# A two-layer mLSTM/attention backbone on one core: TensorE's order written by the program's own plan instead of by the scheduler

## The chip, the core and the metric

The kernel runs on one core of one Trainium2 chip. TensorE (PE) multiplies matrices, VectorE (DVE), ScalarE (ACT) and GpSimd (POOL) work on rows, SyncE (SP) issues the DMAs; each engine has its own list of instructions, and semaphores tie the lists together. Matrix products are accumulated in PSUM, of which the kernel's pools take eight banks; the other tiles lie in SBUF. The metric is the device time of one execution in microseconds, the median of several runs. One further execution was recorded by the profiler; its rows are quoted below.

## The reference

One step through two layers (`DEPTH = 2`), for 128 context tokens and 512 latent tokens with the same weights. D is 1024. Per layer:

```python
sh_a, sc_a, g_a, sh_m, sc_m, g_m = split(silu(cond) @ w_ada + b_ada, 6)
h = x * (1 + sc_a) + sh_a
mq, mk, mv, mo, mg, sq, sk, sv, nq, nk, nv = split(h @ w_in + b_in)
y_ml  = mlstm(mq, mk, mv, mg) normalised, * norm_g * sigmoid(mo)   # 4 heads, two directions
y_swa = softmax with a sink logit over a window and 256 cached keys @ v  # 6 heads, rotary q and k
y_nat = softmax(q k * scale + bias) over an 8x32 patch and 256 cached keys @ v  # 6 heads
x = layer_norm(ALPHA * x + g_a * (concat(y_ml, y_swa, y_nat) @ w_out)) * ln1_g + ln1_b
h = x * (1 + sc_m) + sh_m
x = layer_norm(ALPHA * x + g_m * (square(relu(h @ w_mlp1)) @ w_mlp2)) * ln2_g + ln2_b
```

Context tokens attend to context tokens only. Besides x, the new keys, values and mLSTM states of the context are outputs.

## The kernel before

**Tiling.** The 640 tokens are five tiles of 128 (`NT = 5`; tile 0 is the context). Each large product is made of three matmuls: an operand is split into a rounded part and the remainder (`piece`, L249 to L256: an ACT cast at L254 and a DVE subtraction at L255), and hi·hi, lo·hi and hi·lo are added in PSUM. There are two forms. `gemm_tok` (L258) keeps a tile of the activations stationary, 24 matmuls per token tile into a bank `gtok` (L270). `gemm_feat` (L283) keeps the weights stationary and sends 320 tokens through, twice 24 matmuls into `gfeat` (L301).

**Small matmuls that use part of the array.** These matter for the change. `score` (L751, matmul L758, `s`) works on the two row halves of the array (64x128), one head each. `pv` (L777) turns the softmaxed block `P` with PE transposes (L790, `ptp`), copies the result out of PSUM to `PT`, the first and third group of four on DVE (L799), the second on ACT (L801), and then multiplies it with the values in the two column halves (128x64, L805, `o`), one head each. `ada` (L163, matmul L137, `adaps`) makes the adaLN rows in four column quarters (128x32), four matmuls at a time. In the mLSTM `mls` and `upd` use halves too. The program writes the matmuls of the two heads, and of the four quarters, in turn, so that neighbours work on different parts of the array. An `o` matmul in fp32 is two records of the trace, so a group of 8 shows as 16.

**The plan.** Attention blocks, the mLSTM's blocks and state chain, the transposes of the next stage's input (`to_feat`, L337, transposes L347, `pth`), the outputs of the keys, and `ada` are generators in a queue (`add`, `pump`, `q`, L60 to L95). After every six matmuls of a large product `q` moves a clock of the program forward and takes steps from the queue whose delay has passed. At most two attention blocks are open (`WINDOW`). `drain` empties the queue before the next stage. The order that comes out is only the order in which the code is written: a scheduler then reorders every engine, PE too, by its own priorities.

**Stages of a layer** (`layer`, L1050): the mLSTM's projections (`proj_ml`), three token projections (`proj_tok_a`, `_b`, `_c`), the gates and the mLSTM, then for u = 0, 1, 2 the key and query projections of two heads of neighbourhood attention (`nat`) and of windowed attention (`swa`), each followed by adding five blocks to the queue: 30 softmax blocks a layer. Their projections (`gfeat`) are the filler between the blocks. `tail1` (L937) is the output projection, in `gemm_tok`, with residual and LayerNorm (`ln_add` L920 and L924, `ln_stats` L926 to L934); `to_feat` of each tile follows after a delay of 9.85 in the plan. LayerNorm's gain and bias on the residual (`ln_out`, L968 and L969, whole 1024-wide rows on DVE) come with `ln_late` while the next stage begins. `mlp` (L978) is four chunks of eight `gemm_feat` and two `gemm_tok`. The end of `mlp` of layer 0 crosses to layer 1 in the same way as `tail1` crosses to `mlp`.

**PSUM.** Pool `gp` has four banks for the large products, `sp` one buffer of two banks for scores, `tp` one bank for transposes, `op` one for `o` and the mLSTM.

## Time and profile before

| | us |
|---|---|
| median of 3 runs | 1769.1 (1766.75 to 1769.91) |
| the profiled execution's own time | 1767.37 |
| its span, first instruction to last | 1765.6 |
| PE busy | 1709.0 (97%) |
| DVE busy | 987.7 (56%) |
| ACT busy | 637.6 (36%) |
| TensorE's granted clock, mean | 0.991 |

The stages are found in the trace by the lines of PE's instructions, and the stretches used below follow them: start and first projections of layer 0 up to 200 us, most of its attention 200 to 390, the output projection from 390, its crossing to the MLP 417 to 451, the MLP 451 to 891, the crossing to layer 1 905 to 942, layer 1's attention 1075 to 1265, its crossing 1280 to 1305 and its MLP to 1748. PE counts as busy also while a matmul takes longer than its neighbours of the same shape, so a busy PE is not an engine at its peak: the time between the starts of successive rows tells more than the busy share.

### The profile page before, as it was taken

The numbers are of one execution on the slowest core, as the hardware profiler recorded it, in microseconds if no ns is written. First come the engines' busy times: TensorE is split into PE (matmuls) and PEld (weight loads), VectorE is DVE, ScalarE is ACT, GpSimd is POOL, SyncE is SP. The second block draws the span as 40 slices with busy tenths as digits, with TensorE's granted clock in tenths as the row PEclk, the third lists the DMA queues.
The fourth block names the chain that finished last, engine by engine and source line by source line (L and its number), as shares of the span: only waits on it lengthen the run. The fifth ranks groups of instructions, "written<-read, shape, count | busy, mean of one in ns | idle before, by whom it ended". The sixth has DMA issues, their size and how long they took to land.

```text
span 1765.6 us, 27638 instructions
## 1 busy us (share of the span) xinstructions
PE 1709.0 (97%) x10708; PEld 1441.4 (82%) x10708; DVE 987.7 (56%) x2147; ACT 637.6 (36%) x1410; POOL 182.5 (10%) x152
## 2 busy tenths in 40 slices
PE   6999999999999999999999999999999999999996
PEld 3778777777978978879879798777789898898985
DVE  2368667768533243234384698777784333423438
ACT  2333445534522313213244335565263142231420
POOL 0142000000200201101100411000002011020110
PEclk9999999999999999999999899999999999999998
DMA  8646433233334444434223252211422131221312
GB/s 276 203 129 199 160 98 114 78 119 116 110 106 148 143 137 155 132 109 158 72 89 115 61 170 72 61 59 61 132 92 89 48 108 57 93 78 48 102 43 83
DMA packets 106000, 195.24 MB, mean 111 GB/s; under 512 B 16490, under 2 KB 43114, under 8 KB 100748
## 3 DMA queue, kind: packets, MB, share of 16 engines
q1 hardware_dynamic: 105868, 193.47, 34.1%
q8 instruction: 84, 1.38, 0.3%
q14 instruction: 48, 0.39, 0.1%
HBM read 185.16 MB, written 8.26 MB: 110 GB/s over the span
## 4 chain that ended last, share of the span: by engine, by line
PE 86%; DVE 9%; DMA 2%; issue 1%; ACT 1%; SPq 1%; POOL 0%; DVEq 0%; POOLq 0%
PE gfeat L301 37%; PE gtok L270 32%; PE o L805 4%; PE s L758 4%; PE ptp L790 3%; PE adaps L137 3%; PE mli L609 1%; DVE wst L255 1%; DMA adab<-in_b_ada 1%; DVE res L968 1%; DVE Xt L352 0%; PE pth L347 0%; DMA Dt<-md 0%; DVE res L969 0%; DMA md<-mscr 0%
## 5 line engine op out<-in xcount | busy, mean ns | idle before, releaser
L301 PE MATMUL gfeat<-Xt,wst 128*128 128x320 f32 x4416 | 704.1, 315 | 8.6 <-ACT Xt L211 3.8
L301 PEld LDWEIGHTS gfeat<-Xt,wst 128*128 128x128 f32 x4416 | 655.9, 190 | 47.7 <-issue 25.3
L270 PE MATMUL gtok<-wst,f1T 128*128 128x512 f32 x1920 | 451.5, 395 | 0.0
L270 PEld LDWEIGHTS gtok<-wst,f1T 128*128 128x128 f32 x1920 | 358.7, 188 | 92.8 <-issue 9.2
L255 DVE TENSOR_TENSOR wst<-wrawt,wst 128x512 fp32r<-128x512 f32 (+2 forms) x392 | 271.6, 700 | 270.1 <-ACT wst L254 269.3
L254 ACT CAST wst<-wrawt 128x512 fp32r<-128x512 f32 (+2 forms) x392 | 233.8, 603 | 516.9 <-PE gtok L270 217.0
L920 DVE TENSOR_TENSOR gtok<-gtok,row 128x512 f32<-128x512 f32 x100 | 69.5, 697 | 229.4 <-PE gtok L270 227.6
L997 POOL TENSOR_TENSOR f1T<-f,f1T 128x640 fp32r<-128x640 f32 x64 | 100.8, 1575 | 900.9 <-ACT f1T L996 900.9
L270 PE MATMUL gtok<-wst,Xt 128*128 128x384 f32 (+1 forms) x720 | 129.5, 331 | 1.3 <-DVE wst L255 1.3
L270 PE MATMUL gtok<-wst,yT 128*128 128x512 f32 x480 | 125.1, 405 | 0.0
L270 PEld LDWEIGHTS gtok<-wst,Xt 128*128 128x128 f32 x720 | 114.4, 191 | 9.6 <-issue 3.6
L992 ACT COPY f<-gfeat 128x320 f32<-128x320 f32 x128 | 54.3, 427 | 168.4 <-PE gfeat L301 164.5
L270 PEld LDWEIGHTS gtok<-wst,yT 128*128 128x128 f32 x480 | 86.7, 188 | 22.4 <-issue 4.1
L769 ACT ACTIVATE P<-P,nm 128x512 f32<-128x512 f32 (+2 forms) x120 | 80.6, 673 | 28.8 <-DVE nm L765 16.1
L993 DVE SCALAR_TENSOR_TENSOR f<-f 128x640 f32<-128x640 f32 x64 | 52.7, 824 | 53.2 <-ACT f L992 53.2
L763 DVE TENSOR_REDUCE nm<-P 128x2 f32<-128x1024 f32 (+2 forms) x60 | 66.0, 1107 | 19.6 <-ACT P L892 8.3
L790 PE MATMUL ptp<-ident,P 128*128 128x128 f32 x432 | 71.2, 281 | 2.9 <-DVE P L774 1.8
L137 PE MATMUL adaps<-adaw,cs 128*32 128x512 f32 (+1 forms) x576 | 67.0, 483 | 6.1 <-DVE grow L502 4.2
L790 PEld LDWEIGHTS ptp<-ident,P 128*128 128x128 f32 x432 | 49.0, 140 | 19.2 <-issue 5.7
L350 ACT ACTIVATE val<-pth,affB,affA 128x128 f32<-128x128 f32 x120 | 45.3, 461 | 52.2 <-PE pth L347 51.0
L996 ACT CAST f1T<-f 128x640 fp32r<-128x640 f32 x64 | 46.6, 728 | 31.6 <-DVE f L993 31.6
L799 DVE COPY PT<-ptp 128x512 f32<-128x512 f32 (+1 forms) x72 | 43.1, 599 | 22.4 <-PE ptp L790 22.3
(207 smaller groups left out, 1349.8 us busy)
## 6 DMA issues: line engine op xcount, KB each, us to landing
wrawt<-in_w SPq DMA_DIRECT2D x256, 256.0 KB
adaw<-in_w_ada SPq DMA_DIRECT2D x40, 1024.0 KB
wrawt<-in_w_f SPq DMA_DIRECT2D x56, 256.0 KB
adaw<-in_w_ada SPq DMA_DIRECT2D x32, 256.0 KB
wrawt<-in_w_o SPq DMA_DIRECT2D x32, 256.0 KB
Dt<-md SPq DMA_DIRECT2D x40, 128.0 KB
nbias<-in_nbias SPq DMA_DIRECT2D x18, 256.0 KB
row<-adar SPq DMA_DIRECT2D x8, 512.0 KB
```

Of the source, the lines that this page charges most:

```text
L137: self.nc.tensor.matmul(ps[32 * j : 32 * j + 32, :], lhsT=self.cs[:, k, :], rhs=w[:, j, :], start=(k == 0), stop=(k == 7))
L254: nc.scalar.copy(ws[:, 0, :], raw)
L255: nc.vector.tensor_tensor(out=ws[:, 1, :], in0=raw, in1=ws[:, 0, :].bitcast(F32), op=ALU.subtract)
L270: nc.tensor.matmul(o, lhsT=A[k][:, hl, t * 128 : (t + 1) * 128], rhs=ws[k][:, wl, :], start=(cnt == 0), stop=(cnt == 23),)
L301: nc.tensor.matmul(g[i, h], lhsT=w[i][k // 4][:, wl, (k % 4) * 128 : (k % 4 + 1) * 128], rhs=self.Xt[:, k, hl, h * 320 : (h + 1) * 320], s ...
L758: nc.tensor.matmul(out[h], lhsT=qt[r, a, q0 : q0 + 128], rhs=kf(r, b), start=(i == 0), stop=(i == 2))
L763: nc.vector.tensor_reduce(out=nm[:, 0:2], in_=P[:, :, 0:nk], axis=AX.X, op=ALU.max, negate=True)
L769: nc.scalar.activation(P[:, h, 0:nk], P[:, h, 0:nk], AF.Exp, bias=nm[:, h : h + 1], accum_out=nm[:, 2 + h : 3 + h])
L790: nc.tensor.transpose(pt[:, j, :], P[:, h, i * 128 : (i + 1) * 128], self.ident)
L805: nc.tensor.matmul(o[64 * h : 64 * h + 64, :], lhsT=vf(h, i), rhs=PT[:, h, i, :], start=(i == 0), stop=(i == n - 1))
L920: nc.vector.tensor_tensor(out=o, in0=o, in1=gr[:, qs], op=ALU.mult)
L997: nc.gpsimd.tensor_tensor(out=y[:, 1], in0=f, in1=y[:, 0].bitcast(F32), op=ALU.subtract)
```

## The change

**Order.** The layers are built under `tc.manual_schedule(engines={PE})`: PE keeps the order in which the program writes its instructions. The other engines are still ordered by the scheduler.

**The plan.** `add` and the generators now work with a time at which a step is ready, and `use(engine, us)` books time on a list for ACT, DVE or POOL and returns when the work ends there. `free` waits in the plan until the booked reader of a PSUM bank is done. A step is only written into PE's order after that time. mLSTM blocks run in the order 0, 2, 3, 1, 4 with their normalisation in a group of its own, `fin`. Attention's projections wait for `live` tiles (`until`).

**PSUM and SBUF.** `gp` 4 to 3 banks, `tp` 1 to 2; `upd` and both scores `s2` use `tp`; the pool `ptp` goes and `pp` has four buffers for P and PT.

**Attention.** Every copy to PT is made by ACT. Keys of windowed attention are projected first, `swa` comes ahead of `nat` in each u, `proj_tok_c` after the first `swa`, from which on three attention blocks may be open.

**Output projection.** Its first half goes block by block over y (`by_block`, in the order `YORDER`), tiles 0 to 2 in `gp` and then 3 and 4 in the banks of the scores; there is no drain ahead of it. LayerNorm's gain and bias are made in halves by `ln_half`, at two points within the next stage, in place of `ln_late`. `ada` is spaced 9.5 instead of 12 or 14; the first adaLN bias is loaded ahead of the first weights, and later ones lie in the buffer of the adaLN weights.

The two orders hold the same 9760 matmuls. Counted over them, PE goes from one array shape to another (whole array, row halves, column halves, quarters) 630 times before and 364 times after; in the first stage, up to the first `gtok`, 51 and 9 times. A pair of matmuls on different halves is torn apart by another kind of instruction at 49 places fewer in `o`, about 55 fewer in scores and mLSTM; 8 groups of four of `adaps` are no longer torn.

First place: PE in layer 0's attention, while the projections of u = 1 run. `s` are scores, `ptp` transposes of P, `o` the products with the values, `gfeat` the projections. Before:

```order
L758 MATMUL s<-qkt 128x256 x6
L758 MATMUL s<-kc,qkt 128x256 x6
L301 MATMUL gfeat<-Xt,wst 128x320 x18
L790 MATMUL ptp<-ident,P 128x128 x4
L137 MATMUL adaps<-adaw,cs 32x512 x4
L758 MATMUL s<-qkt 128x256 x6
L790 MATMUL ptp<-ident,P 128x128 x4
L805 MATMUL o<-PT,vt 64x128
L758 MATMUL s<-kc,qkt 128x256 x5
L805 MATMUL o<-PT,vt 64x128 x2
L790 MATMUL ptp<-ident,P 128x128 x4
L805 MATMUL o<-PT,vt 64x128
```

and the same kinds of blocks after:

```order
L375 MATMUL gfeat<-Xt,wst 128x320 x12
L945 MATMUL o<-PT,sv 64x128 x4
L945 MATMUL o<-PT,vc 64x128 x4
L169 MATMUL adaps<-adaw,cs 32x512 x4
L375 MATMUL gfeat<-Xt,wst 128x320 x12
L886 MATMUL s<-qkt 128x128 x6
L375 MATMUL gfeat<-Xt,wst 128x320 x6
L886 MATMUL s<-qkt 128x256 x6
L886 MATMUL s<-kc,qkt 128x256 x6
L375 MATMUL gfeat<-Xt,wst 128x320 x12
L929 MATMUL ptp<-ident,P 128x128 x2
```

The scores, products and adaLN groups stand whole, and the large product comes in runs of 6, 12 or 18 between them.

Second place: PE where layer 0's attention opens. Before, its first block stands among matmuls of the projections:

```order
L156 MATMUL adapt<-ident,adab 128x128 x4
L137 MATMUL adaps<-adaw,cs 32x512 x3
L301 MATMUL gfeat<-Xt,wst 128x320
L758 MATMUL s<-qkt 128x128 x6
L301 MATMUL gfeat<-Xt,wst 128x320 x23
L790 MATMUL ptp<-ident,P 128x128 x2
L301 MATMUL gfeat<-Xt,wst 128x320 x6
```

After, with `mli` the inner products of the mLSTM, `pty` the transposes of its result and `ptko` that of a key output:

```order
L375 MATMUL gfeat<-Xt,wst 128x320 x24
L756 MATMUL pty<-ident,hs 128x128 x2
L886 MATMUL s<-qkt 128x128 x6
L169 MATMUL adaps<-adaw,cs 32x512 x4
L706 MATMUL mli<-vaug,Dt 128x65 x4
L712 MATMUL mli<-mlst,mq 128x130 x4
L706 MATMUL mli<-vaug,Dt 128x65 x4
L863 MATMUL ptko<-ident,kx 128x128
L929 MATMUL ptp<-ident,P 128x128 x2
L886 MATMUL s<-qkt 128x256 x6
L886 MATMUL s<-kc,qkt 128x256 x6
L945 MATMUL o<-PT,sv 64x128 x2
```

From the run of 24 on no large product stands in PE's order for 35 rows, while four softmax blocks and two mLSTM blocks open and close; layer 1 has a like stretch.

Third place: DVE where `tail1` of layer 0 crosses to the MLP; `res` is the residual, `Xt` the next input. Before:

```order
L920 TENSOR_TENSOR gtok<-gtok,row 128x512
L352 TENSOR_TENSOR Xt<-val,Xt 128x4x128
L924 SCALAR_TENSOR_TENSOR res<-res,gtok 128x512
L968 TENSOR_TENSOR res<-res,row 128x1024
L926 BN_STATS bst<-res 128x6
L352 TENSOR_TENSOR Xt<-val,Xt 128x4x128
L932 BN_AGGR bmv<-bst 128x2
L969 TENSOR_TENSOR res<-res,row 128x1024
```

After:

```order
L1084 TENSOR_TENSOR gtok<-gtok,row 128x512
L1088 SCALAR_TENSOR_TENSOR res<-res,gtok 128x512
L426 TENSOR_TENSOR Xt<-val,Xt 128x4x128
L1090 BN_STATS bst<-res 128x6
L291 TENSOR_TENSOR wst<-wrawt,wst 128x512
L1096 BN_AGGR bmv<-bst 128x2
L291 TENSOR_TENSOR wst<-wrawt,wst 128x512
```

The 1024-wide gain and bias are gone from here; their halves (`lnrow`) follow after the last tile's statistics.

The diff, cut:

```diff
+    def use(self, eng, us, after=None):
+        t = (self.T if after is None else after) + 0.08
+        plan = self.te[eng] = [p for p in self.te[eng] if p[1] > self.T - 10.0]
+        while us > 0.01:
+            d = min(us, 0.7)
+            for i, (a, b) in enumerate(plan):
+                if a - t >= d:
+                    break
+                t = max(t, b)
+            else:
+                i = len(plan)
+            plan.insert(i, (t, t + d))
+            t, us = t + d, us - d
+        return t
...
-                        cost, delay = next(s[0])
+                        cost, ready = next(s[0])
                         self.T += cost
-                        s[2] = self.T + delay
+                        s[2] = max(self.T, ready)
...
+    def free(self, *names):
+        while max(self.busy[n] for n in names) > self.T:
+            yield 0.0, max(self.busy[n] for n in names)
...
-    def softmax(self, P, nk, sink=None):
+    def softmax(self, P, nk, f, sink=None):
...
+        f = self.use("V", 0.1 + 1.1 * w, f)
         nc.vector.tensor_reduce(out=nm[:, 0:2], in_=P[:, :, 0:nk], axis=AX.X, op=ALU.max, negate=True)
...
-        yield 0.0, 3.0
+        yield 0.0, f - 0.4 * w
...
-            if gi % 2 == 0:
-                nc.vector.tensor_copy(dst, src)
-            else:
-                nc.scalar.copy(dst, src)
-            yield 0.11 * len(grp), 0.5
+            nc.scalar.copy(dst, src)
+            f = self.use("A", 0.12 + 0.115 * len(grp), self.T + 0.11 * len(grp) + 0.25)
+            self.busy["t"] = f
+            yield 0.11 * len(grp), (f if gi == len(groups) - 1 else f - 0.6 if gi == 1 else self.T) + 0.1
+        yield from self.free("o")
...
+        def finish(t, hs):
...
+            f = self.use("V", 6.0, f)
...
+        bt = self.ada_bias(0, 0, 0, 512)
         load(0)
         nc.sync.dma_start(self.ident, I["ident"])
         self.layer_consts(0)
-        bt = self.ada_bias(0, 0, 0, 512)
...
+            for k in range(7):
+                blocks(k, range(3))
+            self.until(lambda: self.s_left == 0)
...
+            s = self.sp.tile([128, 2, 512], F32, tag="s", name="gtok")
+            g += [s[:, 0], s[:, 1]]
+            for k in range(7):
+                blocks(k, range(3, NT))
+            blocks(7, range(NT))
...
-                    self.add(self.to_feat(r, t, A, B, lg, lb, None), "feat", 9.85)
+                    self.add(self.to_feat(r, t, A, B), "feat", self.use("V", 2.5, f) + (0.5 if t < 3 else 5.0))
...
-            self.gemm_tok([self.Y[k] for k in YORDER], I["w_o"][l, q], 512, ev(q))
+            self.gemm_tok(self.Y, I["w_o"][l, q], 512, ev(q), by_block=q == 0)
...
-    for l in range(L):
-        net.layer(l)
+    with tc.manual_schedule(engines={mybir.EngineType.PE}):
+        for l in range(L):
+            net.layer(l)
```

## Rows read from the trace of the kernel before

**Rows 1.** The page, parts 1 and 4: busy time and chain of waits.

```profile
PE 1709.0 (97%) x10708; PEld 1441.4 (82%) x10708; DVE 987.7 (56%) x2147; ACT 637.6 (36%) x1410; POOL 182.5 (10%) x152
...
PE 86%; DVE 9%; DMA 2%; issue 1%; ACT 1%; SPq 1%; POOL 0%; DVEq 0%; POOLq 0%
```

**Rows 2.** Stretches: length; busy PE, PEld, DVE, ACT, POOL (instructions); clock; DMA share, GB/s.

```profile
0.00:59.00 59.00, 41.78 (x384) 26.11 (x384) 18.10 (x50) 13.97 (x24) 6.54 (x9) 1.00 0.78 260
...
200.00:390.00 190.00, 188.64 (x1417) 139.97 (x1417) 136.92 (x304) 97.30 (x253) 5.97 (x4) 1.00 0.31 102
...
417.00:451.00 34.00, 30.88 (x170) 26.63 (x169) 29.72 (x67) 23.89 (x55) 0.00 (x0) 0.95 0.26 78
451.00:891.00 440.00, 440.00 (x2510) 376.80 (x2509) 166.23 (x244) 121.18 (x219) 51.23 (x33) 1.00 0.39 129
...
905.00:942.00 37.00, 32.59 (x180) 27.72 (x179) 31.71 (x72) 25.62 (x61) 0.56 (x2) 0.95 0.28 98
...
1280.00:1305.00 25.00, 21.88 (x108) 18.10 (x107) 23.45 (x59) 16.80 (x38) 0.00 (x0) 0.93 0.31 97
...
1748.00:1765.60 17.60, 3.53 (x16) 2.51 (x14) 13.86 (x38) 0.00 (x0) 0.00 (x0) 0.66 0.23 90
```

**Rows 3.** Chain of waits: start, length in us, what, within the MLP.

```profile
451.08 44.73 PE gfeat L301 x305
```

**Rows 4.** Timeline of PE, 204 to 218 us: start, length, operation, array shape.

```profile
205.11 0.64 PE L758 MATMUL s<-qkt 64*128 64x256 f32 x6
205.59 0.52 PE L758 MATMUL s<-kc,qkt 64*128 64x256 f32 x6
206.04 2.91 PE L301 MATMUL gfeat<-Xt,wst 128*128 128x320 f32 x18
```

**Rows 5.** Timeline of PE, 278 to 289 us.

```profile
279.05 0.63 PE L758 MATMUL s<-qkt 64*128 64x256 f32 x6
279.61 0.54 PE L805 MATMUL o<-PT,vt 128*64 128x128 f32 x5
...
280.63 0.62 PE L758 MATMUL s<-kc,qkt 64*128 64x256 f32 x6
281.18 1.29 PE L301 MATMUL gfeat<-Xt,wst 128*128 128x320 f32 x7
...
285.32 0.43 PE L805 MATMUL o<-PT,vt 128*64 128x128 f32 x2
285.68 0.50 PE L758 MATMUL s<-qkt 64*128 64x256 f32 x3
```

**Rows 6.** Timeline of PE, 303 to 311 us.

```profile
304.53 2.17 PE L301 MATMUL gfeat<-Xt,wst 128*128 128x320 f32 x13
306.63 1.06 PE L137 MATMUL adaps<-adaw,cs 128*32 128x512 f32 x8
```

**Rows 7.** Waits of PE: what waited, for what, us in total, times, longest.

```profile
PE pth L347 <- ACT val L350: 6.7, 4, 1.9
PE adapt L156 <- DVE adab L148: 5.4, 1, 5.4
...
PE gpm L522 <- DVE gm L519: 3.1, 2, 1.6
```

**Rows 8.** Stretches around layer 1's mLSTM, columns as in rows 2.

```profile
995.00:1000.00 5.00, 3.76 (x26) 3.44 (x25) 1.89 (x4) 3.92 (x13) 4.29 (x5) 0.93 0.04 11
1000.00:1005.00 5.00, 5.00 (x30) 3.44 (x29) 3.13 (x13) 0.42 (x1) 2.63 (x4) 0.50 0.39 105
```

**Rows 9.** One line's instructions, L968: count, duration in ns.

```profile
L968 DVE TENSOR_TENSOR res<-res,row x19: 1212/1218/1226, 420.4 to 1756.2; 128x1024 f32<-128x1024 f32 x19
```

**Rows 10.** Groups by line, 200 to 390 us: busy us, mean ns.

```profile
L763 DVE TENSOR_REDUCE nm<-P 128x2 f32<-128x1024 f32 (+2 forms) x28 | 31.4, 1128 | 8.9 <-ACT P L892 4.0 <-ACT P L831 1.8 <-ACT P L870 1.7
...
L799 DVE COPY PT<-ptp 128x512 f32<-128x512 f32 (+1 forms) x35 | 21.1, 604 | 11.4 <-PE ptp L790 11.3
...
L801 ACT COPY PT<-ptp 128x512 f32<-128x512 f32 x24 | 14.0, 582 | 21.7 <-PE ptp L790 21.5
```

More of the change, by code (lines that the diff above doesn't have):

```diff
@@ L66, in eligible @@
             seen[s[1]] = seen.get(s[1], 0) + 1
-            if seen[s[1]] <= WINDOW[s[1]]:
+            if seen[s[1]] <= WINDOW[s[1]] + (s[1] == "attn" and self.wide):
                 yield s
@@ L558, in gates @@
         self.GB, self.bc, self.W, self.md = GB, bc, W, md
-        yield 0.2, 0.0
+        self.busy["o"] = self.use("V", 1.0, self.T + 0.5)
+        yield 0.2, self.use("A", 1.7, self.busy["o"]) + 0.1
+        while not self.ml_in:
+            yield 0.0, self.T + 1.0
+        self.mlstm(l)
     def mlstm(self, l):
@@ L579, in block @@
         def block(t):
-            hs = sm.tile([128, 4, 64], F32, tag="val", name="hs", bufs=2)
             Dt = self.pp.tile([128, 2, 4, 128], F32, tag="p", name="Dt")
@@ L598, in block @@
                 nc.vector.scalar_tensor_tensor(out=d, in0=sp[:, :, 0:256], scalar=SC, in1=d, op0=ALU.mult, op1=ALU.mult)
-            yield 0.9, 5.0
+            self.busy["s"] = self.use("V", 1.4, max(da, self.T + 0.9))
+            yield 0.7, self.busy["s"] + 0.1
+            while t > 0 and self.chain_p < max(t - 1, 4 - t):
+                yield 0.0, self.T + 0.3
+            while self.hs_live == 2:
+                yield 0.0, self.T + 0.5
+            yield from self.free("s", "o")
+            self.hs_live += 1
+            hs = sm.tile([128, 4, 64], F32, tag="val", name="hs", bufs=2)
             ip = self.sp.tile([128, 2, 512], F32, tag="s", name="mli")
@@ L680, in chain @@
             nc.sync.dma_start(O["new_mlstm_n"][0, l : l + 1].rearrange("o a h e -> o (a h e)"), ce[64:65, :])
+            self.busy["o"] = self.use("A", 0.7, self.T + 2.0)
             yield 1.8, 0.0
-            for t in range(1, 5):
-                self.add(block(t), "attn")
-        self.add(block(0), "attn", 2.0)
-        self.add(chain(), "chain", 2.0)
+        self.live += 1
+        self.chain_p = 0
+        for t in (0, 2, 3, 1, 4):
+            self.add(block(t), "attn")
+        self.add(chain(), "chain")
     def split_qk(self, src, dst):
```

353 lines of the change are left out of this document (237 added, 116 removed).

## The prediction

> **What bounds the kernel now.** I read the page's busy times and chain first, then the stretches by stage, the timeline of PE, its waits, and last the engines that would have to keep up. PE is busy for 97% of the span and 86% of the chain that ended last is its own work; VectorE is next, with 9% of the chain [rows 1]. So the end is set by PE's list: it gets shorter if rows are issued faster, or if PE stands less.
>
> The stages differ. In the MLP PE stands nowhere, 440.00 of 440 us [rows 2], and the chain gives the price of an undisturbed matmul: 305 `gfeat` in 44.73 us, 0.147 us each [rows 3]. In the attention it is just as busy, 188.64 of 190 us in layer 0 [rows 2], but not at that price. Twelve scores in a row take from 205.11 to 206.04, 0.93 us [rows 4]. The same twelve cut by an `o` group take 0.56 (279.05 to 279.61) and 0.55 (280.63 to 281.18), 1.11 in all: one cut, 0.18 more [rows 5]. Thirteen `gfeat` between scores and adaLN take 2.10 us to the next group's start, against 13 times 0.147, 1.91: one visit, 0.19 more [rows 6]. Hence the busy share hides a charge of about 0.19 us for each change of array shape. An `o` pair that stands alone takes more as well: the first of a group, torn off, needs 0.36 us to the next start (two records, 285.32 to 285.68), the other seven (14 records, 279.61 to 280.63) 1.02; if one of them is single at 0.36, a pair costs 0.22 [rows 5].
>
> PE stands for 56.6 us of the span, 1765.6 less 1709.0 [rows 1]: 17.2 in the start (41.78 busy of 59) and 14.1 at the end (3.53 of 17.6), which are chains of other engines and DMAs; 3.1, 4.4 and 3.1 at the three crossings (30.88 of 34, 32.59 of 37, 21.88 of 25) [rows 2]; and the 14.7 that are left in small waits, such as the mLSTM's `gpm` with 3.1 [rows 7].
>
> **The change part by part.** All sums are against the profiled execution, 1767.4 us with a span of 1765.6. The median of the runs is 1.7 us higher; I add that at the end.
>
> *Fewer changes of shape.* 630 become 364, 266 fewer. 42 of them lie in the start, where PE stands anyway; that leaves 224. At 0.19 us: 42.6 us. Transposes beside `gfeat` cost less than scores do; with 0.13 it would be 29 us, with 0.20 45. I take 0.19, since two different kinds of row give it.
>
> *Fewer torn pairs.* A torn `o` pair costs two singles, 0.72, instead of 0.22; about 0.2 to 0.3 of that is the change of shape that is counted already. 49 pairs at 0.21 are 10.3 us. For 55 torn score and mLSTM pairs the trace has no row apart; half of the `o` price, 0.1, gives 5.5 us, bounds 0 and 0.21 each. The 8 torn adaLN groups get nothing up to 1 us each, their eight records' own length [rows 6]; I take 0.5, 4 us. Since first and last matmuls of a visit are priced in both parts, I take 58 of the 62 us. Both ends: 36 to 64.
>
> *Old waits.* PE stands for 10.6 us in the crossings. The cause is seen on DVE: 29.72 busy of 34 us there [rows 2], with passes of 1.22 us over whole rows in it [rows 9], ahead of the statistics and subtractions that PE's transposes and `gfeat` wait for (`pth` on `val` 6.7 us) [rows 7]. The change moves these passes, ten of 1.22 us per crossing, behind the crossing to where DVE has 166 busy of 440 us [rows 2], which hides them. With the small waits that is 25.3 us of standing. After the standing the granted clock is lower: 0.95 in the crossing [rows 2], and at 1000 us 0.50, the 1.2 GHz level, after a stretch with PE busy 3.76 of 5 us [rows 8]. Layer 1's spell lasts some 10 us, those of the crossings some 4 each; half of these 22, 11 us, is lost. Everything gone: 36 us. I book it whole as removed and put what comes back in the next term; if the places stay as they are, 0.
>
> *New waits.* PE's list no longer yields: behind an instruction whose input is late all others stand, the projections too, until ACT or DVE is through. I price four places. First, the stretch with no large product, once in each layer: four softmax blocks and two mLSTM results. DVE, less its copies to PT, has 136.9 − 21.1 = 115.8 us of work for 28 blocks in the attention stretch [rows 2, 10], 4.1 us a block; two mLSTM results at the plan's own 6 us make 28 us. PE needs, per block, 0.93 for twelve scores, 1.18 for eight transposes (estimated at the 0.147 of a `gfeat`), 0.88 for four `o` pairs and 0.57 for three visits, 3.6 us; four blocks are 14 us, the two mLSTM blocks at the plan's 2.4 us 5, and adaLN's groups 1: 20 us. PE waits 8 us, in two layers 16. Second, the last stretch of the attention, where DVE's and ACT's bookings are within 3 or 4 us of PE's: 4 us a layer, 8. Third, the three crossings keep 2 us each for the last tiles' statistics, 6, with 2.5 for the clock after them. Fourth, with three banks the second pair of MLP products waits for a bank once a layer, 0.75 us, 1.5. Sum 34 us. Ends: 8, if the plan's times are right nearly everywhere, and 80, if each of the 60 softmax blocks stands for 0.8 us more.
>
> *The copies to PT.* ACT gets 35 copies more in the stretch, at its own 0.58 us for a full group: 18 us on top of 97.3, while DVE loses 21.1 [rows 2, 10]. Shortened by some 26 us the stretch has 164 us; ACT 115, DVE 116, 71% each. Neither is the bound on average, so the copies cost nothing in the sum; what they cost in a block's latency is a rival.
>
> *The start.* The first adaLN bias lands earlier; PE waited 5.4 us for it [rows 7]. But the DMA share is 0.78 until 59 us [rows 2], the last quarter's weights and its conversion decide when the first stage ends, and in the strict order 72 instead of 31 `gfeat` stand behind the last bias. 41 times 0.147 is 6 us of loss if that bias comes no earlier; 8 us of gain if the 42 changes of shape saved there count in full. I take a gain of 3, ends −8 and +5.
>
> *Nothing:* the end (same work), the closer spacing of adaLN in layer 0's MLP (PE stands nowhere there), `tail1` without a drain (its first tiles take the place of the filler). The cover is the large products' PE time; without it DVE's 2.5 us of statistics per tile would show, as in the crossings.
>
> Sum: −58 −36 +34 −3 = −63. From 1767.4 that is 1704 for a profiled execution, 1706 for a median. Kept as **1705**.
>
> **Rivals.**
>
> *The other engines set the attention.* With two blocks open, and three later, 30 blocks pass through score, maximum, exponent, transposes, copies and `o` one behind the other. If a layer's stretch can't go below the 190 us less half of the 29 us that the first two terms give it, 15 us a layer are lost, and the two openings stand for twice the 8 us, 16 more: 1705 + 46 = 1751. For it: DVE and ACT at 71%, in bursts. Against it: before, at 72% of DVE, PE stood for only 1.4 us in 190.
>
> *All PSUM copies on one engine.* A block's two full groups were copied by DVE and ACT side by side; now the second waits for the first, 0.58 us less the 0.1 us by which DVE's was slower, some 0.48 a block. For 48 such blocks that is 23 us where the copy comes last: 1728. The trace speaks against it, with 71% for each engine. The Trainium skill, "TensorEngine Tiling (Array Packing)", section PSUM Bottleneck, advises to "use both ScalarE and VectorE for PSUM evacuation", against this part of the change; by that rule the 1728 comes true, and no row of the kernel before shows ACT alone.
>
> *A cheaper change of shape.* If part of the 0.19 us is a short wait of the next group for its own input, which the change of order does not remove, 0.1 is left: 224 × 0.1 = 22, half of the pairs 10, so 32 instead of 58: 1731. For it: the scores and products behind such a visit do wait for other engines at times. Against it: the rows with the charge show no wait in front of them [rows 4 to 6].
>
> *Slower: waits at the head of PE's list.* The plan books means, while the scheduler of before could put any `gfeat` in front. If every block stands at its transposes and again at `o`, 120 places, beyond the 34 us, it costs 120 times the delay. Break-even with 63 us is 0.53 us a place; at one reduction of 1.13 us [rows 10] late per place the time is 1705 + 135 = 1840, at 0.75 us 1795. For it: ACT's and DVE's order is still the scheduler's, so the plan's bookings need not be what runs. Against it: the plan's prices are near the rows (a 512-wide copy is booked at 0.58, and takes 0.58), and runs of 6 to 18 `gfeat`, 0.9 to 2.7 us, stand between a block's steps.
>
> **How the numbers follow.** Forecast 0.66; engines set the attention 0.13; one engine's copies 0.05; cheaper change 0.09; slower 0.07. The likeliest one's own range is 1682 to 1728 (the first two terms ±12, new waits −14 to +20, start ±5, not all at once). The range for 8 in 10 reaches down to 1670, the good ends of two terms together, and up to 1748, to just below the second case. A measurement of this kernel can tell about 0.2%, 3.5 us. The forecast, the copies and the cheaper change are faster throughout, the second case nearly so: faster 0.91, within 0.2% 0.02, slower 0.07.
>
> **What would show it.** Right: PE's scores stand as twelve in 0.93 us and its `o` groups without single pairs; the stretches of the two attentions are each about 25 us shorter with the MLP's price of 0.147 unchanged; DVE has no 1.22 us passes in the crossings, and PE's waits for `val` there fall to some 2 us each; the list of PE's waits has new entries for P, PT and the mLSTM's inputs, 16 us of them in the two openings. Wrong: a `gfeat` visit of 6 takes its 0.19 on top and the attentions are not shorter (cheaper change, or the other engines, told apart by PE's standing); waits for `PT` from ACT above all others (one engine's copies); waits of over 60 us for P and PT together, spread over both attentions (slower).

## The result: 0.9% slower

The changed kernel takes 1783.45 us (median of 4 runs, 1781.27 to 1788.49) against 1769.11 us before, a ratio of 1.0087 with a 95% interval of 1.0062 to 1.0112. The prediction said 1705, between 1670 and 1748, and gave "slower" 0.07. The profiled execution has a span of 1783.3 us, 17.7 more than before.

Its page, parts 1 and 4, against [rows 1]:

```profile
PE 1673.5 (94%) x10708; PEld 1453.3 (81%) x10708; DVE 958.7 (54%) x2105; ACT 660.7 (37%) x1482; POOL 187.8 (11%) x152
...
PE 75%; DVE 10%; DMA 5%; ACT 5%; issue 3%; SPq 0%; POOL 0%; DVEq 0%; ACTq 0%; POOLq 0%
```

PE is busy for 35.5 us less than before, as it should be, but it stands for 109.8 us (1783.3 less 1673.5) instead of 56.6. Its own work is 75% of the chain instead of 86%; DMA has gone from 2 to 5%, ACT from 1 to 5%. And the clock is lower. The clock of both kernels, first before, then after (span, mean granted clock):

```profile
core 0: 1765.6 us, clock 0.991
```

```profile
core 0: 1783.3 us, clock 0.968
```

The records show only two levels, full and half. A mean of 0.991 is 2 × 0.009 × 1766 = 32 us at 1.2 GHz; 0.968 is 114 us. Part of that time PE stands anyway. Laid over PE's rows, the clock records have it busy at half clock for 20.4 us before and 92.7 after; if half of that is lost, 10 and 46 us, the clock costs 36 us more. So the rows themselves became cheaper by some 72 us: 35.5 that the page shows, and 36 that the clock took back inside the busy time. That a busy microsecond at half clock does cost half a microsecond is borne out by the table of the experiments.

Two stretches hold the same rows of PE in both kernels: from the start to the first `w2` matmul of layer 0, and from there to the first of layer 1 (length; busy PE, PEld, DVE, ACT, POOL; clock; DMA). Before:

```profile
0.00:495.60 495.60, 466.30 (x3318) 371.51 (x3319) 323.29 (x801) 212.87 (x510) 55.54 (x55) 1.00 0.45 144
495.60:1359.50 863.90, 850.68 (x5280) 720.87 (x5279) 490.63 (x1060) 323.26 (x721) 87.57 (x72) 0.99 0.34 109
```

After:

```profile
0.00:489.30 489.30, 440.99 (x3318) 375.95 (x3319) 305.31 (x776) 224.17 (x546) 55.71 (x55) 0.96 0.44 144
489.30:1378.20 888.90, 841.08 (x5280) 728.18 (x5279) 479.95 (x1043) 335.11 (x757) 92.75 (x72) 0.97 0.33 107
```

The first stretch, with the start and layer 0's attention, gained 6 us; the second, with layer 0's MLP and layer 1's attention, lost 25. PE stands for 48 us in each of them, where it stood for 29 and 13. The rest, layer 1's MLP, takes 406.1 and 405.1 us. The waits of PE in the changed kernel, the largest of the list:

```profile
PE adaps L169 <- DMA adaw<-in_w_ada: 28.3, 8, 7.8
PE gtok L306 <- DVE res L1088: 8.5, 2, 4.8
PE ptp L929 <- DVE P L907: 5.9, 4, 2.6
PE o L945 <- ACT PT L937: 5.7, 8, 2.0
PE o L945 <- DVE yT L963: 5.5, 4, 4.1
PE ptko L863 <- DVE mlst L777: 5.3, 1, 5.3
PE pty L756 <- POOL hs L752: 5.1, 1, 5.1
```

The largest is for the adaLN weights, 28.3 us in eight waits: 16 us in the start, where PE stood for 17 us before as well, the other 12 in layer 0's attention (3.8) and MLP (4.5 and 3.6). In the kernel before, the whole list has 1.8 us for them. Then comes the output projection, and after it many places, a few us each. `pth` for `val`, first in [rows 7], is gone. Stretches that answer to [rows 2]: the start, the opening of layer 0's attention, its main part, the output projection, the crossing to the MLP, the MLP, the crossing to layer 1, the opening of layer 1's attention, its crossing to the MLP, and the end:

```profile
0.00:59.00 59.00, 39.34 (x413) 29.99 (x414) 19.64 (x56) 17.40 (x32) 6.94 (x10) 1.00 0.80 281
183.70:222.00 38.30, 30.33 (x189) 22.28 (x188) 29.14 (x100) 16.06 (x46) 1.61 (x2) 0.73 0.45 148
222.00:384.00 162.00, 153.46 (x1323) 126.75 (x1323) 101.53 (x229) 101.60 (x266) 3.16 (x2) 0.99 0.33 107
384.00:402.00 18.00, 13.17 (x62) 10.24 (x58) 12.96 (x23) 3.36 (x6) 0.00 (x0) 0.91 0.53 163
428.00:451.00 23.00, 22.48 (x152) 21.77 (x151) 20.98 (x47) 15.68 (x37) 0.00 (x0) 1.00 0.50 164
488.00:925.00 437.00, 427.13 (x2333) 357.26 (x2332) 165.26 (x272) 111.33 (x205) 40.14 (x26) 0.98 0.38 125
925.00:960.00 35.00, 31.29 (x195) 29.71 (x194) 29.24 (x69) 19.35 (x47) 0.56 (x2) 0.95 0.52 171
1064.00:1113.00 49.00, 36.50 (x239) 31.09 (x238) 39.38 (x137) 19.25 (x56) 2.26 (x3) 0.72 0.16 50
...
1312.00:1340.00 28.00, 26.02 (x172) 24.71 (x171) 24.16 (x55) 18.98 (x45) 0.00 (x0) 1.00 0.35 102
...
1766.00:1783.30 17.30, 3.60 (x16) 2.58 (x14) 14.00 (x38) 0.00 (x0) 0.00 (x0) 0.71 0.23 91
```

Here the places show. The crossing to the MLP is filled, 22.48 of 23 us at full clock, where it was 30.88 of 34. But the MLP, which stood nowhere, now stands for 9.9 us; the output projection for 4.8 of 18; and in the two openings PE stands for 8.0 and 12.5 us and runs at 0.73 and 0.72.

### The profile page after: what moved, and what is told of

Same layout as the page of the kernel before. It is cut to its first block, busy times and chain, and to the rows that moved or that the text cites. A ratio compares the mean times of both kernels' runs of the same rounds, so it can differ in the third digit from the quotient of the medians.

```text
span 1783.3 us, 27709 instructions
## 1 busy us (share of the span) xinstructions
PE 1673.5 (94%) x10708; PEld 1453.3 (81%) x10708; DVE 958.7 (54%) x2105; ACT 660.7 (37%) x1482; POOL 187.8 (11%) x152
## 4 chain that ended last, share of the span: by engine, by line
PE 75%; DVE 10%; DMA 5%; ACT 5%; issue 3%; SPq 0%; POOL 0%; DVEq 0%; ACTq 0%; POOLq 0%
PE gtok L306 34%; PE gfeat L375 31%; PE adaps L169 2%; ACT P L900 2%; PE o L945 2%; PE ptp L929 2%; DMA adaw<-in_w_ada 2%; DVE nm L893 2%; PE s L886 1%; PE mli L706 1%; DVE P L907 1%; DVE wst L291 1%; ACT PT L937 1%; DMA nbias<-in_nbias 1%; DMA adab<-in_b_ada 1%
## 5 line engine op out<-in xcount | busy, mean ns | idle before, releaser
L375 PE MATMUL gfeat<-Xt,wst 128*128 128x320 f32 x4416 | 688.1, 315 | 3.0 <-ACT f L1170 1.3
L1084 DVE TENSOR_TENSOR gtok<-gtok,row 128x512 f32<-128x512 f32 x100 | 69.4, 697 | 226.9 <-PE gtok L306 226.7
L306 PE MATMUL gtok<-wst,yT 128*128 128x512 f32 x480 | 120.3, 406 | 8.5 <-DVE res L1088 8.5
L306 PE MATMUL gtok<-wst,Xt 128*128 128x384 f32 (+1 forms) x720 | 122.1, 324 | 1.8 <-ACT wst L290 1.6
L306 PEld LDWEIGHTS gtok<-wst,yT 128*128 128x128 f32 x480 | 90.7, 193 | 30.4 <-DVE res L1088 9.4
L169 PE MATMUL adaps<-adaw,cs 128*32 128x512 f32 (+1 forms) x576 | 60.0, 513 | 29.0 <-DMA adaw<-in_w_ada 28.3
L929 PE MATMUL ptp<-ident,P 128*128 128x128 f32 x432 | 65.5, 290 | 7.1 <-DVE P L907 5.9
L937 ACT COPY PT<-ptp 128x512 f32<-128x512 f32 (+1 forms) x120 | 60.9, 541 | 23.8 <-PE ptp L929 23.1
L1174 ACT CAST f1T<-f 128x640 fp32r<-128x640 f32 x64 | 46.6, 728 | 35.5 <-DVE f L1171 35.5
```

The costliest lines, as they stand in the source:

```text
L169: self.nc.tensor.matmul(ps[32 * j : 32 * j + 32, :], lhsT=self.cs[:, k, :], rhs=w[:, j, :], start=(k == 0), stop=(k == 7))
L306: nc.tensor.matmul(o, lhsT=A[YORDER[k] if A is self.Y else k][:, hl, t * 128 : (t + 1) * 128], rhs=ws[k][:, wl, :], start=(k == 0 and hl + ...
L375: nc.tensor.matmul(g[i, h], lhsT=w[i][k // 4][:, wl, (k % 4) * 128 : (k % 4 + 1) * 128], rhs=self.Xt[:, k, hl, h * 320 : (h + 1) * 320], s ...
L929: nc.tensor.transpose(pt[:, j, :], P[:, h, i * 128 : (i + 1) * 128], self.ident)
L937: nc.scalar.copy(dst, src)
L1084: nc.vector.tensor_tensor(out=o, in0=o, in1=gr[:, qs], op=ALU.mult)
```

## The experiments

Theory 1: the rows became cheaper as forecast, and the strict order gave that back, as waits behind late inputs at the head of PE's list and as the lower clock after them. Theory 2: the rearranged banks, buffers and copies cost the time, whatever orders PE. Besides, single places and the price of a change of shape were tested by themselves. The numbers of all runs, in us, by medians, by three stretches of the profiled execution (start to layer 0's first `w2` matmul, from there to layer 1's, and the rest), and by PE's busy time in it, with the part of that in which the records give half clock:

| kernel | median | ratio to before (95%) | stretches | PE busy, at half clock |
|---|---|---|---|---|
| before | 1769.1 | | 495.6, 863.9, 406.1 | 1709.0, 20.4 |
| changed | 1783.5 | 1.0087 (1.0062 to 1.0112) | 489.3, 888.9, 405.1 | 1673.5, 92.7 |
| 1 scheduler orders PE | 1733.7 | 0.9791 (0.9773 to 0.9809) | 480.5, 847.0, 405.3 | 1664.7, 34.9 |
| 2 before, strict order | 1913.2 | 1.0820 (1.0793 to 1.0847) | 556.5, 945.3, 406.3 | 1705.9, 137.5 |
| 3 bias buffer | 1762.3 | 0.9962 (0.9946 to 0.9977) | 487.0, 873.0, 405.1 | 1669.1, 84.3 |
| 4 copies on two engines | 1774.4 | 1.0024 (1.0013 to 1.0035) | 490.6, 875.6, 406.1 | 1666.0, 76.5 |
| 5 edits 1 and 3 | 1719.4 | 0.9727 (0.9702 to 0.9752) | 472.0, 842.9, 405.3 | 1661.6, 29.9 |
| 6 addition on GpSimd | 1781.1 | 1.0075 (1.0048 to 1.0101) | 489.0, 882.6, 406.2 | 1671.0, 85.9 |
| 7 filled | 1799.1 | 1.0175 (1.0159 to 1.0191) | 505.1, 887.5, 405.1 | 1713.9, 49.6 |
| 10 edits 1, 3, 4, 6 | 1715.9 | 0.9708 (0.9693 to 0.9723) | 469.1, 841.5, 405.4 | 1658.4, 22.9 |
| 11 edits 3, 4, 6 | 1755.6 | 0.9930 (0.9912 to 0.9948) | 483.0, 865.5, 405.8 | 1660.0, 63.9 |
| 12 half filled | 1783.9 | 1.0076 (1.0056 to 1.0095) | 495.9, 882.8, 405.5 | 1688.5, 61.9 |
| 13 later bookings | 1793.8 | 1.0134 (1.0111 to 1.0158) | 493.6, 893.0, 405.8 | 1676.4, 82.1 |

The last column prices the clock. The changed kernel and the kernels 3, 4, 6 and 11 have nearly the same rows in nearly the same order, and PE is busy for 1660.0 to 1673.5 us in them; with half of the time at half clock taken off, all five come to 1627 or 1628. The three kernels with the scheduler's order (1, 5 and 10) come to 1647, the kernel before to 1699.

### 1 and 2: who orders PE

The changed kernel without the strict order:

```diff
-    with tc.manual_schedule(engines={mybir.EngineType.PE}):
-        for l in range(L):
-            net.layer(l)
+    for l in range(L):
+        net.layer(l)
```

> The changed kernel with one thing undone: the scheduler orders TensorE again, all other parts stay. Theory 1 (TensorE's own rows became cheaper by some 60 us, and the strict order gives that back as waits behind late inputs, 110 us of standing against 57, and as time at the lower clock after each of them): the waits shrink to about 60 us and the torn rows return, so 1755 to 1775. Theory 2 (the rearranged banks, buffers and copies cost the time, whatever orders TensorE): no better than the changed kernel, 1780 to 1800.

It takes 1733.7 us, 50 us less than the changed kernel and 36 less than the kernel before, better than both theories said. Its page, its clock, and the second stretch:

```profile
PE 1664.7 (96%) x10708; PEld 1435.5 (83%) x10708; DVE 956.3 (55%) x2105; ACT 659.8 (38%) x1482; POOL 188.8 (11%) x152
```

```profile
core 0: 1732.8 us, clock 0.985
```

```profile
480.50:1327.50 847.00, 828.32 (x5281) 715.07 (x5280) 475.92 (x1043) 334.95 (x757) 93.74 (x72) 0.99 0.34 112
```

PE stands for 68.1 us instead of 109.8, and for 19 instead of 48 in the second stretch; the time at half clock is 2 × 0.015 × 1733 = 52 us instead of 114. Of the 50.5 us between the two spans, 41.7 are standing, 8.8 busy time. The 8.8 are a difference: 29 us are won back from the clock (34.9 us of busy time at half clock instead of 92.7), and some 20 are lost to rows that are torn again. So theory 2 falls: under the scheduler's order the other parts of the change are a gain of 36 us together. Theory 1 holds on where the time went, but misjudged how many torn rows return. Counted as in the section on the change, with 630 changes of shape in the kernel before and 364 in the changed one, this kernel has 462; at 0.20 us (experiments 8 and 9) the 98 more would be those 20 us. Most of the plan's runs thus stay whole under the scheduler.

The reverse, the kernel before with the strict order put around its layers:

> The kernel before with one thing done: TensorE keeps the program's order, with the old plan of fixed delays. Theory 1: rows become cheaper here too (its order has 736 rows against 986 of the kernel before), but the fixed delays of the old plan are further from the other engines than the bookings, so the waits grow at least as in the changed kernel: 1785 to 1830. Theory 2 (the strict order is harmless, the other parts cost): faster than before, 1720 to 1750.

1913.2 us, 8% slower and far above the 1785 to 1830 that theory 1 expected, though it has only 340 changes of shape, the fewest of all. Its page and its first wait:

```profile
PE 1705.9 (89%) x10708; PEld 1467.3 (77%) x10708; DVE 998.8 (52%) x2147; ACT 638.6 (33%) x1410; POOL 181.4 (10%) x152
```

```profile
PE ptp L790 <- DVE P L774: 44.1, 30, 3.4
```

PE stands for 202 us (1908.1 less 1705.9): transposes are written where a fixed delay of 3.0 says that the softmax is through, and it isn't. Its rows did become cheaper: less half of the time at half clock, PE is busy for 62 us less than before. The strict order costs 144 us with the old plan and 50 with the bookings. The bookings are what makes it bearable; they don't make it better than the scheduler's.

### 3: the buffer of the adaLN bias

```diff
-        if l + i == 0:
-            bt = self.sm.tile([128, n], F32, tag="val", name="adab", bufs=2)
-        else:
-            bt = self.adp.tile([128, n], F32, tag="aw", name="adab")
+        bt = self.sm.tile([128, n], F32, tag="val", name="adab", bufs=2) if l + i == 0 else self.wraw.tile([128, n], F32, tag="raw", name="adab")
```

> The changed kernel, with the adaLN bias in a buffer of the weights' staging pool instead of in the only buffer of the adaLN weights; TensorE's order is the same to the row. Theory 1: the next group's first weights were loaded only after the bias had left the buffer, and TensorE waited for them 3.8, 4.5 and 3.6 us, with some 20 us at half clock after these waits: both go, 22 us in all, 1762. Rival (the loads were late because the queue of DMAs was full, not because of the buffer): within 4 us of the changed kernel.

1762.3 us, 21.1 less; 22 were expected. The chain in the changed kernel shows the mechanism in the MLP, from 566 us on (start, length, what):

```profile
566.66 12.51 PE gfeat L375 x84
579.17 0.45 PE adapt L191 x4
...
579.63 5.23 DMA adaw<-in_w_ada
...
585.00 1.60 PE adaps L169 x8
```

The pool `adp` has one buffer. The bias lies in it until PE has transposed the sum, at 579.6; only then can the next group's first weights be loaded, 5.23 us, and the plan puts their matmuls directly behind. With the bias elsewhere, the load runs ahead and the same place reads

```profile
576.72 0.60 PE L188 MATMUL adapt<-ident,adab 128*128 128x128 f32 x4
...
578.12 1.07 PE L169 MATMUL adaps<-adaw,cs 128*32 128x512 f32 x8
```

with no wait. Of the 28.3 us for the adaLN weights the start's are left:

```profile
PE adaps L169 <- DMA adaw<-in_w_ada: 16.1, 5, 7.8
```

So the rival, a full queue of DMAs, falls. The page of this kernel and its clock:

```profile
PE 1669.1 (95%) x10708; PEld 1451.8 (82%) x10708; DVE 958.9 (54%) x2105; ACT 660.3 (37%) x1482; POOL 188.0 (11%) x152
```

```profile
core 0: 1765.1 us, clock 0.969
```

Of the 18.2 us between the two spans 13.8 are standing (96.0 instead of 109.8) and 4.4 busy time. The clock's mean is unchanged, but PE is busy at half clock for 84.3 us instead of 92.7, which accounts for 4.2 of the 4.4.

### 4: copies to PT

```diff
-            nc.scalar.copy(dst, src)
-            f = self.use("A", 0.12 + 0.115 * len(grp), self.T + 0.11 * len(grp) + 0.25)
+            if gi % 2 == 0:
+                nc.vector.tensor_copy(dst, src)
+                f = self.use("V", 0.15 + 0.135 * len(grp), self.T + 0.11 * len(grp) + 0.25)
+            else:
+                nc.scalar.copy(dst, src)
+                f = self.use("A", 0.12 + 0.115 * len(grp), self.T + 0.11 * len(grp) + 0.25)
```

> The changed kernel with the copies to PT alternately on VectorE and ScalarE, as before, and booked so in the plan. If one engine for all copies was the cost (the rival of the prediction), 10 to 23 us faster, 1760 to 1773, with the 5.7 us of waits of the products for PT gone. If VectorE is the later of the two engines in the stretches without a large product, within 5 us of the changed kernel or up to 10 us slower.

1774.4 us, 9.0 less, just short of the range that the rival expected; all of it lies in the second stretch (875.6 instead of 888.9), none in the first. Here the measurement goes with the Trainium skill, "TensorEngine Tiling (Array Packing)", section PSUM Bottleneck, which advises to use both engines for PSUM. But its reason, the wait for the copies, isn't what went: PE's waits for PT are longer here, 10.6 and 2.1 us for `o` instead of 5.7:

```profile
PE o L949 <- DVE PT L938: 10.6, 10, 3.0
...
PE o L949 <- ACT PT L941: 2.1, 5, 0.7
```

The waits for yT became shorter (for `o` 1.2 instead of 5.5 us, for `s` 1.7 instead of 3.6), and the one for `hs`, 5.1 us, left the list. In sum PE stands for 106.3 us, 3.5 less, and is busy for 7.5 less:

```profile
PE 1666.0 (94%) x10708; PEld 1446.0 (82%) x10708; DVE 989.0 (56%) x2177; ACT 629.8 (36%) x1410; POOL 188.8 (11%) x152
```

```profile
core 0: 1772.3 us, clock 0.972
```

The clock accounts for all of the busy time: at half clock PE is busy for 76.5 us instead of 92.7, and half of the difference is 8.1. The edit also moves the plan's bookings, and with them its order, so that the copies and the order aren't told apart: the gain is measured, and what in the edit brings it is open.

### 6: one small addition

The sum of the forget bias in the bias rows of each layer, by `nc.gpsimd` instead of `nc.vector`; layer 1's is the one that matters here.

> The changed kernel with one small addition (the forget bias into layer 1's bias rows) made by GpSimd instead of VectorE. In the trace of the changed kernel it stands in VectorE's list in the middle of layer 0's output projection, waits there for its DMA until 391.8 us, and the evacuations behind it release a PSUM bank late, for which TensorE stands 4.8 us and then runs 3.4 us at half clock. If this is the cause: 6 us faster, 1777. If VectorE would be late there anyway (weights for the second half come by the same queue): within 2 us.

1781.1 us, 2.3 less, as the second of the expectations; the intervals of both kernels overlap. The reading was right and the price wrong. The changed kernel's chain, where PE waits 4.83 us in the output projection:

```profile
384.91 6.83 DMA brow<-in_brow
...
391.83 0.06 DVE brow L454
```

An addition for layer 1, ready to be hoisted because its rows lie in the four-buffer pool `pp` now, stands in VectorE's list ahead of the evacuations and waits for its load. With it gone, the weights of the projection's second half are next. VectorE's subtraction for each of them waits for ScalarE's cast, and the cast waits until `gtok` gives a weight buffer back:

```profile
389.44 0.62 ACT L290 CAST wst<-wrawt 128x512 fp32r<-128x512 f32 x1 [0.78 <-PE gtok L306]
```

```profile
390.09 0.69 DVE L291 TENSOR_TENSOR wst<-wrawt,wst 128x512 fp32r<-128x512 f32 x1 [0.71 <-ACT wst L290]
390.70 1.29 DVE L1084 TENSOR_TENSOR gtok<-gtok,row 128x512 f32<-128x512 f32 x2
```

The first evacuation, `L1084`, starts at 390.70 instead of 392.55 in the changed kernel, and PE's wait is 3.5 us. The block-by-block form keeps all eight weight buffers to its end, so that those weights come late in any case, and lets five tiles finish within 15 matmuls, so that their evacuations queue.

### 8 and 9: the price of a change of shape

The diff, cut:

```diff
...
+                            if self.probe is not None:
+                                nc.tensor.matmul(self.probe, lhsT=self.ident[0:64, :], rhs=self.ident[0:64, :], start=True, stop=True)
                             self.q(self.six(320))
...
```

with 128 in place of 64 in the first, in the last three chunks of layer 1's MLP.

> The changed kernel with 168 further matmuls of the identity, 128x128 on the whole array, one after every six gfeat in the last three chunks of layer 1's MLP, where nothing else runs on TensorE. They compute nothing that is read. Their own price: 0.1 to 0.3 us each, 17 to 50 us in all.

> The same 168 further matmuls, but on the upper 64 rows of the array, so that each goes into another shape and back. If a change of shape costs 0.19 us, as the prediction had it, two changes make each 0.38 us dearer than with the whole array, 64 us in all. If 0.19 is the price of in and out together: 32 us. If the charge was the wait of neighbours: under 8 us.

1812.0 and 1887.0 us (one run each): 75 us apart, 0.45 a matmul. In the timelines, whole array first, then half:

```profile
1451.29 0.38 PE L383 MATMUL probe<-ident 128*128 128x128 f32 x2
1451.43 1.12 PE L376 MATMUL gfeat<-Xt,wst 128*128 128x320 f32 x6
1452.38 0.38 PE L383 MATMUL probe<-ident 128*128 128x128 f32 x2
```

```profile
1453.47 0.48 PE L383 MATMUL probe<-ident 64*128 64x128 f32 x2
1453.89 1.15 PE L376 MATMUL gfeat<-Xt,wst 128*128 128x320 f32 x6
1454.96 0.48 PE L383 MATMUL probe<-ident 64*128 64x128 f32 x2
```

A round of six `gfeat` and one probe takes 1.09 us with the whole array and 1.49 with half of it. Two changes cost 0.40 us, 0.20 each, with nothing else on PE and no wait. The 0.19 of the prediction stands, and the "cheaper change" falls. Only the change between the whole array and half of its rows was probed; that column halves and quarters cost the same isn't shown by itself.

### 7 and 12: filling the openings

Transposes of the identity wherever the plan jumps over a gap of PE ahead of a projection of the attention, mostly in the two openings; the diff, cut:

```diff
         while not done():
+            gap = min(s[2] for s in self.eligible()) - self.T
+            if fill and gap > 0.25:
+                if pd is None:
+                    pd = self.gp.tile([128, 512], F32, tag="g", name="fill")
+                for _ in range(int(gap / 0.125)):
+                    self.nc.tensor.transpose(pd[:, 0:128], self.ident, self.ident)
...
-        self.until(lambda: self.live < 5 and (mode == "nk" or self.y_live < 8))
+        self.until(lambda: self.live < 5 and (mode == "nk" or self.y_live < 8), True)
```

> The changed kernel with transposes of the identity added to TensorE's list in the two stretches that have no large product, as many as fill the plan's own gaps there (0.125 us each; about 30 us of them in all). They compute nothing that is read, so TensorE has strictly more to do. If the clock after a wait is a cost of its own, the lower clock in these stretches (20 us at half rate in layer 0, 27 in layer 1) gets shorter: up to 15 us faster than the changed kernel, 1768 to 1780. If standing alone costs and the clock is only a companion: the additions delay the blocks, 1785 to 1800.

1799.1 us, 15.6 more, within the range of the second expectation. But each transpose is two records 0.11 us apart at full clock, 0.22 us together, so that the 578 records added some 63 us, twice what was meant; the clock rose to 0.982. With `gap / 0.25`:

> As the filled kernel, with half as many transposes: there each took 0.24 us, twice what the plan's gaps were divided by, so 69 us were added where 30 were meant, and it was 16 us slower than the changed kernel while the time at half clock fell from 112 to 65 us. If the clock after a wait is a cost that filling can win back, now 1765 to 1778. If TensorE's standing there is set by VectorE's chain, whatever the clock: 1782 to 1792, with the time at half clock lower again.

1783.9 us: 31 us of work more (282 records, 181 of them in the openings), and no time more or less. The clock is 0.976 instead of 0.968, and PE is busy at half clock for 61.9 us instead of 92.7, which gives back 15 us. But only 14 of the 31 us fell into time in which PE stood before (it stands for 95.8 us now), and the other 17 used the gain up. The two openings, each from the last `gfeat` ahead of it to the first behind it, in the changed kernel and in this one:

```profile
187.50:219.70 32.20, 24.23 (x148) 16.23 (x146) 24.16 (x85) 14.03 (x40) 1.61 (x2) 0.69 0.43 146
1069.90:1107.40 37.50, 25.00 (x159) 20.10 (x158) 32.47 (x120) 16.07 (x48) 2.26 (x3) 0.68 0.14 44
```

```profile
187.50:223.20 35.70, 27.70 (x212) 20.93 (x211) 24.06 (x84) 13.83 (x40) 1.60 (x2) 0.81 0.39 133
1075.20:1109.20 34.00, 29.41 (x277) 25.74 (x275) 31.52 (x115) 14.22 (x43) 2.18 (x3) 1.00 0.16 48
```

Layer 1's opening runs at full clock and is 3.5 us shorter, layer 0's is 3.5 us longer. The time lies in the range of the second expectation. Its reason fits layer 1's opening, where VectorE is busy for 31.5 of the 34.0 us; it doesn't fit layer 0's, with 24.1 of 35.7. So the clock after a wait is a cost of its own, but filling wins it back only at the price of the filler.

### 13: later bookings

```diff
-                        s[2] = max(self.T, ready)
+                        s[2] = max(self.T, ready + (1.0 if s[1] == "attn" else 0.0))
```

> The changed kernel with 1.0 us added to the time at which each step of an attention or mLSTM block is ready in the plan. If the waits behind P, PT and yT come from bookings that are too early, they shrink where projections can fill the time (layer 0 from 240 us, layer 1 from 1120): 10 to 20 us faster, 1763 to 1773. If the stretches without a large product decide, they get longer by 1 us a step: 1785 to 1810.

1793.8 us, 10.3 more, within what was expected if the stretches without a large product decide. Its first wait of attention:

```profile
PE o L945 <- ACT PT L937: 8.3, 17, 1.6
```

Waits for PT became more, 17 instead of 8. So the waits are not simply bookings that are too early everywhere: moving all of them by the same 1.0 us lengthens both stretches (493.6 and 893.0). A likely reason, not shown by itself, is that each block stays open longer while only two or three may be open. Whether better bookings would remove the waits stays open.

### 5, 10 and 11: together

> The changed kernel with the scheduler ordering TensorE, and the adaLN bias in the staging pool: both single edits together. If the two losses are independent, the 50 us of the scheduler's order and what is left there of the bias's 21 us: that kernel still waits 16.3 us for adaLN weights, 7.6 of it at the start, so 5 to 9 more, 1725 to 1729. If the scheduler hides the shared buffer by itself: 1732 to 1736.

1719.4 us: 14.3 less than with the scheduler alone, more than expected.

> The same three edits with TensorE's order still the program's. If the single gains of the changed kernel (21, 9 and 2 us) are independent: 1751. If the plan's errors only come out at the next place: 1757 to 1765. In neither case does it reach the scheduler's order.

1755.6 us, 27.9 less than the changed kernel where the single gains sum to 32.4. That is between the two expectations, so the gains are nearly independent; and it is 0.7% less than before with the strict order kept.

> The scheduler's order with the three single edits together: the adaLN bias in the staging pool, the copies to PT on two engines, the small addition on GpSimd. If the copies' 9 us come from fewer waits at the head of TensorE's list, the scheduler hides most of them: 1714 to 1720, against 1719 without the last two. If they come from the engines' work itself: 1708 to 1711.

1715.9 us, a ratio of 0.9708 (0.9693 to 0.9723): faster than both kernels. Copies and addition win 3.5 us on top of the 5th kernel, where the intervals touch, against 11.3 singly in the strict order: most of what they won there is not to be had again from the scheduler's order.

## Why the prediction was wrong

**The bound and the price of a change of shape: right.** PE's list set the end before; 0.19 us for a change was read off three rows, and the probe measured 0.20. With the start the prediction took off 61 us; busy time and clock together show some 72. The start itself came out: the first `gtok` begins at 58.9 us instead of 63.3, where a gain of 3 was booked.

**Old waits: right at the crossings, wrong in the rest.** The three crossings stand for 0.5, 3.7 and 2.0 us instead of 3.1, 4.4 and 3.1, and `pth` on `val` left the list. The small waits did not go away; others took their places.

**New waits: the step that failed.** It priced four places at 31.5 us of standing. The crossings came out, 6.2 us for the 6 booked, and so did the bank of the MLP (1.3 us of `gfeat` on `f`, 1.5 booked). The openings came near, 8.0 and 12.5 us for 8 each; 3.8 us of layer 0's are the wait for adaLN weights, but with these in time (experiment 3) PE still stands for 7.5 us there, for P above all. The rest of the attention stands for 8.5 and 10.5 us (222 to 384 and 1113 to 1272), where 4 each were booked for its last stretch. What it missed besides is the two places that it costed at nothing, and the many small waits that it took as gone. The closer adaLN was waved off with "PE stands nowhere there": that is a statement on the kernel before, and the edit moved the bias into the only buffer of the next weights. The three waits are 11.9 us, and the edit that removes them gave 21.1 us, measured. `tail1` without a drain was to be covered by "its first tiles"; PE waits 8.5 us there, on evacuations that come five at a time. The mLSTM's state chain and the middle of the attention have waits of 2 to 5 us for `mlst`, yT and P that no term held. All in all PE stands for 109.8 us where 56.6 − 25.3 + 31.5 = 62.8 were forecast: 47 more.

**The clock after the waits: a gain was booked, and it became a loss.** The prediction took 11 us of old loss as gone and booked 2.5 as new, a gain of 8.5 us. PE's busy time at half clock rose instead from 20.4 to 92.7 us, and the loss by 36. In the kernel before the half clock came after a few waits at the crossings [rows 2, 8]; the row was read there and priced for the crossings alone, though the new waits bring the same wherever they are: the openings run at 0.73 and 0.72, the output projection at 0.91.

**The sum.** The forecast for the profiled execution was 63 us less, and it took 17.7 more. Of these 81 us 47 are standing and 45 the clock (36 lost where 8.5 were to be won); the rows, some 11 us cheaper still than forecast, gave a part back.

**The rival that came true** is the last, waits at the head of PE's list, with a chance of 0.07: it came true in its name, but not in its places. It let the blocks of the attention stand at their transposes and at `o`, with waits of over 60 us for P and PT together as its sign; PE's waits for P and PT are under 20 us. The standing lies in many places, and the clock adds nearly as much. One argument for it was good: the other engines' order is still the scheduler's, so the plan's bookings need not be what runs. Against the other engines as a bound stood that PE waited for only 1.4 us in 190 before; but that was under an order that could bring any `gfeat` forward, the very thing that the change takes away. A row measured under a flexible order says nothing on what a fixed one would wait for.

**What was attributed wrongly.** The forecast gave the whole gain of whole groups to the strict order. The kernel with the scheduler's order has 462 changes of shape against 630, stands for 68 us, and is 36 us faster than before. Of the 72 us by which the rows became cheaper it has 51 (1699 to 1647 at full clock), so most of what was wanted comes without forcing the order. How much of its 36 us is due to the order in which the program is written, and how much to banks, buffers and LayerNorm's halves, no run separates.

**The other engines as the bound:** layer 1's opening behaves so (VectorE busy for 32.5 of 37.5 us), layer 0's less (24.2 of 32.2), and the whole attention does not. The main part of layer 0's, 222 to 384 us, has DVE at 63% and ACT at 63%, with PE busy 95%. The rival of one engine's copies, 23 us, came out smaller: undoing that part (experiment 4) gives 9.0 us in all.

## What to carry to other kernels

Before an engine is taken from the scheduler and given a fixed order, every input at which its list can stand has to be priced, those of rare and cheap rows too (a bias load, a state update), since everything behind them stands as well; a kernel's standing under a flexible order is no measure of it. Writing the program in a good order and leaving the scheduler in charge may give most of the gain: try that alone first. And where a tile moves into another pool, ask who else takes buffers from that pool and how far ahead they could load until then.

## What the runs showed of the hardware

A change of TensorE's array shape between neighbouring matmuls costs 0.20 us each way, measured by a probe of 128x128 that went from the whole array to 64 rows and back (1.49 against 1.09 us a round); other shapes weren't probed. The granted clock fell to half in stretches after PE had stood: 114 us of 1783 with 110 us of standing, 32 of 1766 with 57, 187 of 1908 with 202 (from the means 0.968, 0.991 and 0.951); but it doesn't follow the sum of standing alone, since 109 of 1765 came with 96 (0.969) and 99 of 1772 with 106 (0.972). What it costs is half of the time in which PE is busy at half clock: with that taken off, five kernels with nearly the same order, busy for 1660.0 to 1673.5 us, agree within about 1 us. Filling with 31 us of idle work gave 15 us of that back and moved the time by 0.4 us.
